# Slots of three SBUF pools set 4128 bytes apart instead of 4096

## The chip, the cores and the metric

The kernel runs on one core of a Trainium2 chip. The metric is device time in microseconds of one execution. The kernel before has a median of 1593.42 us over three runs.

## The reference

One layer of a streaming-encoder trunk for 512 tokens of width 1024. The parts that matter here:

```python
h    = rms_norm(x, norm_mix_gain)
proj = h @ w_in                              # 1024 x 3328, split into head groups
mixed = concat(stick_breaking(...), hgrn2(...), memory_attention(...))
x = x + mixed @ w_out
x = x + peer_ffn(rms_norm(x, norm_ffn_gain), ...)

def peer_ffn(h, w_query, sub_keys, expert_u, expert_v):   # per token, 8 heads
    q      = h @ w_query
    scores = einsum('bthcd,hcnd->bthcn', q, sub_keys)     # two lists of 128 keys
    top 16 of each list, top 16 of their sums -> expert_idx (of 16384), gate = softmax
    act = gelu(einsum('btd,bthkd->bthk', h, expert_u[expert_idx]))
    return einsum('bthk,bthkd->btd', gate * act, expert_v[expert_idx])
```

## The kernel before

The tokens lie in four tiles of 128. Tile 0 (`GT`) takes its experts by indirect DMA: 128 gathers of U rows and 128 of V rows. Tiles 1 to 3 (`DENSE`, 384 tokens) compute all 16384 experts densely, in 128 blocks of 128 experts: `u_mm` (line 1381) multiplies h2 by a block of U into the PSUM tile `ua`, and later `v_mm` (line 1456) multiplies the gated activations by a block of V into six PSUM banks `pin`.

Nearly every large product is made of three matmuls (`mm3`, line 419). Each float32 operand is split into a high part, rounded to the fp32r format by a copy, and a low part, the remainder: hi x hi, hi x lo and lo x hi are summed in PSUM. A U block (tile `ex`, 128x1024) is split by ScalarE into `xhi` and by VectorE into `xlo`; a V block likewise. The trace names a matmul's operands as moving operand first, stationary operand second: `ua<-h2hi,xhi` streams h2hi past the weights xhi, `pin<-xhi,whi` streams xhi past the weights whi.

SBUF tiles come out of tagged pools of equal slots (`slot`, line 284, and `t2`, line 302). The names that the change touches:

- `page`, tag "a2", 16 slots: gathered rows (`row`), gelu outputs (`gel`), one-hot tiles (`oh`), staging (`stg`), the running sum `xg`, and the early V splits.
- `hpage`, tag "h", 8 slots: the split activations (`hhi`, `hlo`, `mxh`, `mxl`, `h2hi`, `h2lo`).
- `wpage`, tag "w4", 8 slots: the split weights (`whi`, `wlo` of the projections; `xhi`, `xlo` of U and V blocks).

Not touched: `raw`, tag "raw", 7 slots (blocks as they land, `ex` and `w`); `t2`, 8 slots of 2048 bytes (`w`, `whi`, `wlo` of the gated activations, `shi` and `slo` of the stick-breaking part); `big3`, 2 slots (`G`); and the constants `ntri` and `nones`.

The program's list of allocations gives the byte addresses within a partition. In the kernel before, a2 starts at 20576, t2 at 86112, h at 102496, raw at 135264, w4 at 165984, b3 at 198816; the last tile ends at 228064. ntri lies at 17216 and nones at 18240. Modulo 4096, every a2, h and raw slot starts at 96, every w4 slot at 2144, and the t2 slots at 96 and 2144 in turn.

The order of the work is written out by the program: generators (`Threads`) are run against a clock model (`Pace`), and the engines take their instructions in the order in which the generators emit them. `Pace` reads an operand's tensor name and its offset within its tensor, not its address.

Of the kernel before, what the change touches and what calls it, by code (L numbers as in the profile page):

```python
# [20 lines left out]
P = 128  # L21
# [9 lines left out]

NPG, NRAW, NW4, NT2 = 16, 7, 8, 8
NBIG = 2
NSB = 3
QL = 2

# [228 lines left out]
def tile_trunk_layer(ctx: ExitStack, tc: tile.TileContext, x, mem, w_in, w_kv, w_out, w_query,  # L265
# [7 lines left out]
    sb = ctx.enter_context(tc.tile_pool(name="sb", bufs=1))  # L273
    ps = ctx.enter_context(tc.tile_pool(name="ps", bufs=1, space=PSUM))
    ctx.enter_context(tc.manual_schedule())
    uid = [0]

    def bank(name="pb", dt=F32, shape=None):
# [2 lines left out]
        PSUMS.add(b.tensor.name)  # L281
        return b

    def slot(tag, bufs):
        def make(shape, dt=F32, name="pg"):
            uid[0] += 1
            t = sb.tile(shape, dt, name=f"{name}{uid[0]}", tag=tag, bufs=bufs)
            return t
        return make

    page = slot("a2", NPG)
    hpage = slot("h", 8)
    wpage = slot("w4", NW4)
    raw = slot("raw", NRAW)
    big3 = slot("b3", NBIG)

# [1290 lines left out]

    for _ in range(NSB):
        th.add(sbreak())
# [66 lines left out]
```

## Time and profile before

| | us |
|---|---|
| median of three runs | 1593.42 (1592.74 to 1597.09) |
| the profiled execution's own time | 1591.55 |
| span of the profiled execution, first to last instruction | 1589.8 |
| TensorE busy | 1555.6 |
| VectorE busy | 1260.6 |
| ScalarE busy | 751.2 |
| mean granted TensorE clock, share of 2.4 GHz | 0.994 |

The profiled execution took 1.75 us more than its span, and 1.9 us less than the median. The time up to 472 us goes to projections, attention, recurrence, output projection and query; from 472 to 1059 us the U blocks run, with the top-k selection and the building of gate tables beside them; from 1059 to 1586 us the V blocks run. A line in the rows below, L204, is the helper that records every operation, so groups go by tiles. A matmul's duration in the rows contains its pipeline; the distance from one start to the next is what it takes of TensorE's time.

### The profile page before, as it was taken

Reading aid. Unit: us, or ns where it says so; the run is one execution under the profiler, and the core shown is the slowest. Engines: PE = TensorE matmul, PEld = TensorE weight load, DVE = VectorE, ACT = ScalarE, POOL = GpSimd, SP = SyncE. Lnnn points to the kernel's source line nnn. Section 1 sums busy time; section 2 is a strip of 40 time slices with the busy share of each in tenths; the row PEclk is TensorE's granted clock in tenths of the full one; section 3 lists DMA queues with packets and bytes.
Section 4 is the critical chain, followed back from the end, with each engine's and each line's share of the span. In section 5 each row is a group of like instructions: output and inputs, shape, how many; then the busy total and the mean of one; then the engine's idle time right before and its main releaser. Section 6 shows DMA issues by size and latency. Waiting matters only on the chain.

```text
span 1589.8 us, 25664 instructions
## 1 busy us (share of the span) xinstructions
PE 1555.6 (98%) x9359; PEld 1424.8 (90%) x9359; DVE 1260.6 (79%) x2527; ACT 751.2 (47%) x1427; POOL 351.9 (22%) x340
## 2 busy tenths in 40 slices
PE   6999998999999999999999999999999999999998
PEld 5998998889999999999999999988888888888887
DVE  5465568795887888788877878768898889888886
ACT  5422258854443456576566755533333333333332
POOL 3000000000061211121112110134344444344430
PEclk9999999999999999999999999999999999999999
DMA  6232102264297868889889898899999999999992
GB/s 252 80 106 80 54 28 89 97 226 135 86 336 260 267 224 297 272 290 319 263 280 299 277 295 262 296 402 408 408 408 407 395 377 382 387 390 380 364 380 77
DMA packets 163951, 422.72 MB, mean 266 GB/s; under 512 B 13552, under 2 KB 62704, under 8 KB 163824
## 3 DMA queue, kind: packets, MB, share of 16 engines
q1 hardware_dynamic: 67824, 236.51, 40.8%
q0 software_dynamic: 36864, 134.23, 23.0%
q10 hardware_dynamic: 59136, 50.34, 9.9%
q8 instruction: 73, 1.20, 0.3%
q14 instruction: 54, 0.44, 0.1%
HBM read 366.50 MB, written 54.53 MB: 265 GB/s over the span
## 4 chain that ended last, share of the span: by engine, by line
PE 93%; DVE 4%; ACT 2%; issue 1%; DMA 0%; SPq 0%; ACTq 0%; DVEq 0%
PE ua L204 34%; PE pin L204 33%; PE pf L204 5%; PE pt L204 4%; PE qf L204 4%; PE gb L204 3%; PE op L204 2%; PE hs L204 2%; PE qp L204 1%; PE sz L204 1%; ACT se L204 1%; PE qs L204 1%; DVE tka L204 1%; PE so L204 1%; PE nt L204 0%
## 5 line engine op out<-in xcount | busy, mean ns | idle before, releaser
L204 DVE TENSOR_TENSOR xlo<-ex,xhi 128x1024 fp32r<-128x1024 f32 x256 | 312.8, 1222 | 96.9 <-issue 45.1
L204 POOL DMA_INDIRECT row<-in_u_rows_dram,eidx x128 | 156.5, 1223 | 928.3 <-ACT sct L204 408.2
L204 PE MATMUL ua<-h2hi,xhi 128*128 128x384 f32 x1024 | 349.6, 341 | 0.0
L204 PE MATMUL ua<-h2hi,xlo 128*128 128x384 f32 x1024 | 343.5, 335 | 0.0
L204 PE MATMUL ua<-h2lo,xhi 128*128 128x384 f32 x1024 | 343.1, 335 | 0.0
L204 ACT ACTIVATE whi<-w 128x384 fp32r<-128x384 f32 (+1 forms) x201 | 141.0, 718 | 344.1 <-DVE w L204 325.2
L204 PE MATMUL pin<-xhi,whi 128*128 128x512 f32 x768 | 299.9, 390 | 1.5 <-ACT whi L204 1.5
L204 PE MATMUL pin<-xlo,whi 128*128 128x512 f32 x768 | 299.9, 391 | 1.2 <-DVE xlo L204 1.2
L204 PE MATMUL pin<-xhi,wlo 128*128 128x512 f32 x768 | 299.9, 391 | 0.0
L204 ACT ACTIVATE xhi<-ex 128x1024 fp32r<-128x1024 f32 x256 | 268.7, 1051 | 24.7 <-ACT stg L204 6.5
L204 DVE TENSOR_TENSOR wlo<-w,whi 128x384 fp32r<-128x384 f32 (+1 forms) x200 | 156.3, 796 | 110.7 <-ACT whi L204 56.7
L204 POOL DMA_INDIRECT row<-in_v_rows_dram,eidx x128 | 178.3, 1393 | 253.5 <-DVE w L204 129.2
L204 PEld LDWEIGHTS ua<-h2lo,xhi 128*128 128x128 f32 x1024 | 192.6, 188 | 0.0
L204 PEld LDWEIGHTS ua<-h2hi,xhi 128*128 128x128 f32 x1024 | 192.4, 188 | 0.0
L204 PEld LDWEIGHTS ua<-h2hi,xlo 128*128 128x128 f32 x1024 | 192.3, 188 | 0.0
L204 PEld LDWEIGHTS pin<-xhi,whi 128*128 128x128 f32 x768 | 144.7, 188 | 31.7 <-ACT whi L204 1.8
L204 PEld LDWEIGHTS pin<-xlo,whi 128*128 128x128 f32 x768 | 144.6, 188 | 31.5 <-DVE xlo L204 1.5
L204 PEld LDWEIGHTS pin<-xhi,wlo 128*128 128x128 f32 x768 | 144.6, 188 | 30.0
L204 DVE SCALAR_TENSOR_TENSOR xg<-row,wgt,xg 128x1024 f32<-128x1024 f32 x128 | 163.9, 1280 | 0.8
L204 DVE CUSTOM_DVE_ANT_0 row<-row,xr 128x1024 f32<-128x1024 f32 x128 | 155.2, 1218 | 4.6 <-DMA row<-in_u_rows_dram,eidx 4.6
L204 ACT ACTIVATE gel<-ua 128x384 f32<-128x384 f32 x128 | 62.8, 491 | 190.4 <-PE ua L204 189.2
L204 ACT ACTIVATE oh<-oh,gpg 128x128 f16<-128x128 f16 x256 | 84.3, 436 | 16.2 <-DVE sct L204 5.2
(255 smaller groups left out, 2281.1 us busy)
## 6 DMA issues: line engine op xcount, KB each, us to landing
ex<-in_u_t_dram SPq DMA_DIRECT2D x128, 512.0 KB, 4.7
ex<-in_v_rows_dram SPq DMA_DIRECT2D x128, 512.0 KB, 10.4
gel<-gel ACTq DMA_DIRECT2D x64, 384.0 KB, 4.1
gd<-stg ACTq DMA_DIRECT2D x48, 512.0 KB, 6.9
G<-gd SPq DMA_DIRECT2D x48, 512.0 KB, 6.9
gel<-gel SPq DMA_DIRECT2D x64, 384.0 KB, 9.9
w<-in_w_query_dram SPq DMA_DIRECT2D x28, 512.0 KB, 4.7
w<-in_w_in_dram SPq DMA_DIRECT2D x26, 512.0 KB, 4.9
```

The costliest lines, as they stand in the source:

```text
L204: r = fn(*args, **kw)
```

## The change

A slot of the pools a2, h and w4 is now a tile of 128 partitions x (4096 + 32) bytes. The tile that the caller asked for is the first part of it, reshaped to the caller's shape. Other pools stay as they were.

```diff
 NBIG = 2
+SLOT = 4096
 NSB = 3
...
+    PAD = {"w4": 32, "h": 32, "a2": 32}
+
     def slot(tag, bufs):
         def make(shape, dt=F32, name="pg"):
             uid[0] += 1
-            t = sb.tile(shape, dt, name=f"{name}{uid[0]}", tag=tag, bufs=bufs)
+            if tag not in PAD:
+                return sb.tile(shape, dt, name=f"{name}{uid[0]}", tag=tag, bufs=bufs)
+            n, z = 1, mybir.dt.size(dt)
+            for c in shape[1:]:
+                n *= c
+            t = sb.tile([P, SLOT // z + PAD[tag] // z], dt, name=f"{name}{uid[0]}", tag=tag, bufs=bufs)[:, :n]
+            if len(shape) > 2:
+                ax = "abcd"[:len(shape) - 1]
+                t = t.rearrange(f"p ({' '.join(ax)}) -> p {' '.join(ax)}", **dict(zip(ax[1:], shape[2:])))
             return t
         return make
```

The three pools have 32 slots together, so 1024 bytes of each partition are added.

## Rows read from the trace of the kernel before

**Rows 1.** From the page: busy time of each engine with its share of the span, and the chain of work that ended last, by engine and by line.

```profile
PE 1555.6 (98%) x9359; PEld 1424.8 (90%) x9359; DVE 1260.6 (79%) x2527; ACT 751.2 (47%) x1427; POOL 351.9 (22%) x340
...
PE 93%; DVE 4%; ACT 2%; issue 1%; DMA 0%; SPq 0%; ACTq 0%; DVEq 0%
PE ua L204 34%; PE pin L204 33%; PE pf L204 5%; PE pt L204 4%; PE qf L204 4%; PE gb L204 3%; PE op L204 2%; PE hs L204 2%; PE qp L204 1%; PE sz L204 1%; ACT se L204 1%; PE qs L204 1%; DVE tka L204 1%; PE so L204 1%; PE nt L204 0%
```

**Rows 2.** Busy time by stage, in three stretches: length, busy time of each engine with its instructions, then granted TensorE clock, DMA share (mean busy share of the 16 DMA engines) and GB/s.

```profile
0.00:472.00 472.00, 445.62 (x3199) 417.94 (x3200) 321.02 (x799) 230.61 (x456) 39.55 (x100) 0.99 0.37 129
472.00:1059.00 587.00, 585.58 (x3859) 572.97 (x3857) 475.36 (x1157) 332.75 (x716) 108.53 (x93) 1.00 0.85 284
1059.00:1586.00 527.00, 524.44 (x2304) 433.84 (x2304) 464.19 (x572) 187.86 (x256) 203.77 (x147) 1.00 0.95 369
```

**Rows 3.** What TensorE waited for from 472 to 1586 us: total us, times, longest.

```profile
PE pin L204 <- ACT whi L204: 1.5, 1, 1.5
PE pin L204 <- DVE xlo L204: 1.2, 1, 1.2
PE qs L204 <- ACT qT L204: 0.4, 1, 0.4
```

**Rows 4.** Groups of TensorE instructions with shapes kept apart: count, then busy us and mean ns of one. Each of the four stands for three groups of its name with the same count (hi x hi, hi x lo, lo x hi).

```profile
L204 PE MATMUL ua<-h2hi,xhi 128*128 128x384 f32 x1024 | 349.6, 341 | 0.0
L204 PE MATMUL pin<-xhi,wlo 128*128 128x512 f32 x768 | 299.9, 391 | 0.0
L204 PE MATMUL pf<-hhi,whi 128*128 128x512 f32 x128 | 50.8, 397 | 0.0
L204 PE MATMUL qf<-h2hi,whi 128*128 128x384 f32 x112 | 38.2, 341 | 0.0
```

**Rows 5.** Timeline of TensorE in the V blocks: start us, duration us. From the first of these rows to the last there are 15 matmuls, one to a row.

```profile
1399.63 0.39 PE L204 MATMUL pin<-xhi,whi 128*128 128x512 f32 x1
1399.86 0.39 PE L204 MATMUL pin<-xlo,whi 128*128 128x512 f32 x1
1400.08 0.39 PE L204 MATMUL pin<-xhi,wlo 128*128 128x512 f32 x1
...
1402.80 0.39 PE L204 MATMUL pin<-xhi,wlo 128*128 128x512 f32 x1
```

**Rows 6.** The same in the U blocks: 19 matmuls from the first row to the last.

```profile
699.73 0.34 PE L204 MATMUL ua<-h2lo,xhi 128*128 128x384 f32 x1
699.90 0.33 PE L204 MATMUL ua<-h2hi,xlo 128*128 128x384 f32 x1
700.08 0.34 PE L204 MATMUL ua<-h2hi,xhi 128*128 128x384 f32 x1
...
702.85 0.33 PE L204 MATMUL ua<-h2lo,xhi 128*128 128x384 f32 x1
```

**Rows 7.** Timeline of TensorE in the stick-breaking part: a matmul that streams slo past the constant ntri, and the one that follows at once with the constant nones. First two of the seven pairs with 512 columns that run back to back, then two of the six with 384 columns.

```profile
284.84 0.39 PE L204 MATMUL sz<-slo,ntri 128*128 128x512 f32 x1
285.07 0.39 PE L204 MATMUL sz<-slo,nones 128*128 128x128 f32 x2
...
305.10 0.39 PE L204 MATMUL sz<-slo,ntri 128*128 128x512 f32 x1
305.33 0.39 PE L204 MATMUL sz<-slo,nones 128*128 128x128 f32 x2
...
252.61 0.34 PE L204 MATMUL sz<-slo,ntri 128*128 128x384 f32 x1
252.78 0.40 PE L204 MATMUL sz<-slo,nones 128*128 128x128 f32 x2
...
269.03 0.34 PE L204 MATMUL sz<-slo,ntri 128*128 128x384 f32 x1
269.21 0.39 PE L204 MATMUL sz<-slo,nones 128*128 128x128 f32 x2
```

**Rows 8.** From the views by tile: duration in ns (shortest/median/longest), first and last start in us, and shape, of operations that read and write slots of the three pools, and of the weight loads of ua.

```profile
L204 DVE TENSOR_TENSOR xlo<-ex,xhi x256: 1205/1220/1300, 468.4 to 1572.9; 128x1024 fp32r<-128x1024 f32 x128
L204 ACT ACTIVATE xhi<-ex x256: 1039/1047/1089, 467.3 to 1571.0; 128x1024 fp32r<-128x1024 f32 x128
L204 DVE SCALAR_TENSOR_TENSOR xg<-row,wgt,xg x128: 1272/1280/1287, 1152.7 to 1575.3; 128x1024 f32<-128x1024 f32 x128
L204 PEld LDWEIGHTS ua<-h2hi,xhi x1024: 187/188/192, 472.7 to 1056.7; 128*128 128x128 f32 x171
L204 PEld LDWEIGHTS sz<-slo,ntri x32: 187/190/331, 173.0 to 309.3; 128*128 128x128 f32 x32
```

**Rows 9.** The DMA: from the page, the queue of the indirect gathers (packets, MB, share of 16 engines' span), and DMA issues with their size and median us to landing; then the gathers issued in the V stretch (POOL, x147), with the DMA share and GB/s of that stretch at the end of the line.

```profile
q0 software_dynamic: 36864, 134.23, 23.0%
ex<-in_v_rows_dram SPq DMA_DIRECT2D x128, 512.0 KB, 10.4
gel<-gel SPq DMA_DIRECT2D x64, 384.0 KB, 9.9
row<-in_v_rows_dram,eidx POOLq DMA_INDIRECT x128, 8.4
...
1065.00:1586.00 521.00, 195.83 (x155) 203.77 (x147) 1.00 0.95 368
```

**Rows 10.** What VectorE waited for from 1065 to 1586 us: total us, times, longest.

```profile
DVE wlo L204 <- PE pin L204: 50.5, 84, 1.1
DVE xr L204 <- PE pin L204: 4.8, 1, 4.8
```

## Prediction

> **What bounds the kernel now.** I read the page's busy times and its chain of waits first, then the stages, then TensorE's own waits, and last the distance between matmul starts. TensorE is busy for 98% of the span and makes up 93% of the chain that ended last; ua and pin alone are 67% of it [rows 1]. The stage view says the same of each stage: 585.6 of 587 us in the U blocks, 524.4 of 527 in the V blocks [rows 2]. In these 1114 us TensorE waited 3.1 us for anybody [rows 3]. So two questions decide this change: does the distance between two matmul starts move, and does some other engine or the DMA slow down so far that TensorE has to wait?
>
> **The distance now.** In the V blocks 14 steps take 1402.80 - 1399.63 = 3.17 us, 226.4 ns each [rows 5]. In the U blocks 18 steps take 3.12 us, 173.3 ns each [rows 6]. The 128 more columns cost 53.1 ns, 0.415 ns a column, which is the 2.4 GHz level of the clock. 512 columns are then 212.4 ns, and 14.0 ns of each matmul is a fixed part. That fixed part is all that a better layout could take from TensorE's stream. It is the same for whichever of the three products comes next, and for 384 and 512 columns within the 10 ns of the rows.
>
> **The change, part by part.**
>
> *Instructions.* None is added, removed or moved. The planner reads a tensor's name and offsets within a tensor; a view that starts at offset 0 of a slightly longer row gives it the same spans. Operands stay contiguous within a partition, so each keeps its shape and each DMA keeps its 4096-byte pieces. Cost 0. The three pools grow by 32 x 32 = 1024 bytes, to an end at 229088; no slot is given up for it.
>
> *Where operands lie.* Before, the starts of any two tiles in a2, h, w4, t2 and raw differ by multiples of 2048 bytes, and the slices that one matmul takes differ by multiples of 512. After, slot j of h and slot m of w4 differ, modulo 512, by 256 + 32(m - j): all sixteen phases occur. t2 moves by 512, raw by 768 and b3 by 1024 bytes as a whole. What this can change is a collision between two reads of one engine or between two engines, if such collisions depend on the phase.
>
> *TensorE, moving operand against weight load.* The trace before has matmuls at another phase. ntri and nones lie 736 and 1760 bytes past the phase of slo's slot, 224 modulo 512, which is 7 x 32 and one of the phases that the change brings in. With 384 columns six pairs start 0.17 or 0.18 us apart (mean 0.173), as in ua; with 512 columns seven pairs start 0.23 us apart against 0.226 [rows 7, 5, 6]. The weight load takes 188 ns for the ua blocks and 190 for ntri at the median [rows 8]. So the fixed part stands there too, undiminished. Bounds for the cost: below, the whole 14.0 ns goes away; above, the 3.6 ns by which the 512-column pairs stand over pin are real. Groups of three with 384 or 512 columns are 3 x (1024 + 768 + 128 + 112) = 6096 matmuls [rows 4]: 6096 x 14.0 = -85 us. Above: the 512-column ones are 3 x (768 + 128) = 2688, so 2688 x 3.6 = +10 us. I take 0, because the 384-column pairs are the nearest row and show no difference either way; a 512-column pair is followed by a 128-column matmul, not by its like.
>
> *VectorE and ScalarE.* Their operations on these slots meet every timing of TensorE's reads and of the DMA's writes, since the engines are not in step. If collisions cost anything at some phases, durations would spread. They don't: xg takes 1272 to 1287 ns over 128 times, xhi 1039 to 1089 and xlo 1205 to 1300 over 256 each [rows 8]. xlo reads two operands at one phase, xg reads two slots of one pool. The room for a gain is the median less the shortest, 15 ns x 256 for xlo, 4 us in all on an engine that waits for pin in 84 places [rows 10], so nothing at the end. Upward, VectorE is busy for 464 of 527 us in the V blocks [rows 2]: its operations could grow by 13% before it set the pace. The cover that hides them is this slack.
>
> *DMA.* Gathers and gelu tiles land in a2 at phases that now vary by slot. The DMA share in the V blocks is 0.95 [rows 2, 9], so the cover is thin. The moved transfers there are 147 gathers of 134.23 MB / 256 = 0.524 MB (77 MB) and 64 returns of gel of 0.393 MB (25 MB), against 521 us x 368 GB/s = 192 MB [rows 9]: 53%. The share reaches 1.0 when the moved transfers take 0.05 / 0.95 / 0.53 = 10% longer. The mean packet of the gather queue takes 0.23 x 16 x 1589.8 us / 36864 = 159 ns, index packets included [rows 9]; 10% is 16 ns on each. No row shows a transfer to another phase. I take 0: every slot stands at byte 96 modulo 256 before, and after it only one of every eight does, the others lying around it, so there is no aligned state to lose.
>
> The Trainium skill, page "DMA: Bandwidth & Descriptors", section "How a descriptor splits into AXI transactions", speaks against slots off a 256-byte boundary: transactions must start at such a boundary, and bytes below the start are fetched and dropped. By it, a 4096-byte piece at 96 modulo 256 counts 131 beats of 32 bytes, and the new slots count 128 to 135, 131.5 on average (an estimate from that page's rule). That would be 0.4% on the moved transfers, far below the 10% above, so by the rule the sum stays the same. The trace before, with one phase only, can't confirm it.
>
> **The sum.** 0 against the profiled execution's own 1591.55 us (span 1589.8 and 1.75 around it). Its three runs have a median 1.9 us above; against that median I forecast 1593.4 us.
>
> **The rivals.**
>
> *Faster: the fixed part is a collision.* If the 14 ns stand for weight loads and streams that meet because all starts are multiples of 512 apart, phases spread over sixteen values remove most of it. All of it gives 1593.4 - 85 = 1508; one tenth gives 1585. For it: the fixed part is the same everywhere, as a locked collision would be. Against it: ntri and nones at 224 modulo 512 show the same distance [rows 7].
>
> *Slower: phases that collide come in.* The mechanism is TensorE's two reads, in the V blocks and the first projections, 2688 matmuls of 512 columns. Price 3.6 ns each, +10 us, 1603. It decides against me from 1.8 ns each on (4.8 us, 0.3%). For it: the 0.23 us of the seven 512-column pairs. Against it: the 384-column pairs.
>
> *Slower: the DMA becomes the bound.* From 10% on the moved transfers. At 20% the share would be 0.95 x (1 + 0.53 x 0.20) = 1.05, 5% of 521 us, +26 us, 1619. For it: the share of 0.95. Against it: the phases before are no better ones.
>
> *The change does nothing to the addresses* (the allocator rounding slots to another step). The starts before are multiples of 32, so a step of 4128 can be given; if not, the time is again 1593.
>
> **How the numbers follow.** No change, including the last rival: 0.80. Faster collision: 0.10, spread from 1585 down to 1508. TensorE collision: 0.07. DMA: 0.03. Two measurements of this kernel can be told apart from about 0.3%, 4.8 us: 1588.6 to 1598.2. So faster 0.10, same 0.80, slower 0.10. The range takes in the forecast with its scatter and the priced slower bound: 1587 to 1603. Outside it lie the strong forms of the faster case and the DMA case, together under 2 in 10.
>
> **What would show it.** In the profile after, pin steps of 226 to 227 ns and ua steps of 173 to 174 ns would show the main step right; a pin step of 213 or one of 230 would show a rival, and so would a step that changes from block to block with the slot. Medians of xlo, xhi and xg more than 20 ns off would show the engines' reads do care. A DMA share near 1.0 in the V blocks, with landings far over 10 us and TensorE waiting for xhi or xlo, would show the DMA rival. A changed instruction count or new waits on TensorE would break the first step. I would be wrong above all if the phase matters only at differences other than 224 modulo 512, since the trace before holds only 0 and that one.

## The result, and the profile after

The changed kernel takes 1608.45 us (median of four runs, 1606.69 to 1610.27) against 1593.36 us (now also a median of four): a ratio of 1.009, 95% interval 1.0076 to 1.0104. That is 15.1 us slower, and outside the predicted range of 1587 to 1603. The forecast was no change.

Each engine has as many instructions as before (25664 in all), and from 472 us on TensorE waits for the same things; only addresses differ. So the two traces can be laid side by side stage by stage. The view by tile gives the first and the last start of the U and V matmuls; first the kernel before:

```profile
L204 PE MATMUL ua<-h2hi,xhi x1024: 333/335/424, 472.8 to 1056.9; 128*128 128x384 f32 x171
L204 PE MATMUL pin<-xhi,whi x768: 387/390/628, 1059.1 to 1583.9; 128*128 128x512 f32 x192
L204 PE MATMUL pin<-xhi,wlo x768: 388/390/629, 1061.1 to 1584.4; 128*128 128x512 f32 x192
```

and the same lines of the kernel after:

```profile
L205 PE MATMUL ua<-h2hi,xhi x1024: 331/337/427, 474.3 to 1062.9; 128*128 128x384 f32 x171
L205 PE MATMUL pin<-xhi,whi x768: 387/394/628, 1065.1 to 1600.7; 128*128 128x512 f32 x192
L205 PE MATMUL pin<-xhi,wlo x768: 387/393/628, 1067.4 to 1601.2; 128*128 128x512 f32 x192
```

From the first ua to the first pin it was 1059.1 - 472.8 = 586.3 us and is 1065.1 - 474.3 = 590.8, +4.5. From the first to the last pin it was 1584.4 - 1059.1 = 525.3 and is 1601.2 - 1065.1 = 536.1, +10.8. What lies ahead of the U blocks grew by 1.5 us, the tail not at all (5.4 us in both). Together 16.8 us, the difference of the two spans (1606.6 and 1589.8); the medians differ by less, 15.1, because the profiled execution of the kernel before was 1.8 us under its median. The V blocks carry two thirds of it.

What TensorE waited for from 472 to 1606 us in the kernel after:

```profile
PE pin L205 <- ACT whi L205: 1.5, 1, 1.5
PE pin L205 <- DVE xlo L205: 1.2, 1, 1.2
PE qs L205 <- ACT qT L205: 0.4, 1, 0.4
```

These are the same three waits as in [rows 3], to the tenth. Nobody keeps TensorE waiting for longer; its own matmuls follow one another more slowly. The timeline of the V blocks, 16 matmuls from the first row to the last, and of the U blocks, 11 matmuls (start us, duration us):

```profile
1399.98 0.39 PE L205 MATMUL pin<-xhi,whi 128*128 128x512 f32 x1
1400.21 0.39 PE L205 MATMUL pin<-xlo,whi 128*128 128x512 f32 x1
1400.45 0.39 PE L205 MATMUL pin<-xhi,wlo 128*128 128x512 f32 x1
...
1403.46 0.39 PE L205 MATMUL pin<-xhi,whi 128*128 128x512 f32 x1
```

```profile
701.08 0.34 PE L205 MATMUL ua<-h2lo,xhi 128*128 128x384 f32 x1
...
702.84 0.34 PE L205 MATMUL ua<-h2hi,xlo 128*128 128x384 f32 x1
```

15 steps of pin in 3.48 us are 232.0 ns each, against 226.4 in [rows 5]; 10 steps of ua in 1.76 us are 176.0 ns, against 173.3 in [rows 6]. The other engines and the DMA did not move. Durations by tile (shortest/median/longest, ns), then the stage view from 1059 to 1586 us, the V stretch of [rows 2], whose first 6 us are still U blocks here (DMA share and GB/s are the last two numbers):

```profile
L205 DVE TENSOR_TENSOR xlo<-ex,xhi x256: 1203/1219/1227, 469.9 to 1589.4; 128x1024 fp32r<-128x1024 f32 x128
L205 ACT ACTIVATE xhi<-ex x256: 1041/1047/1086, 468.8 to 1587.5; 128x1024 fp32r<-128x1024 f32 x128
L205 DVE SCALAR_TENSOR_TENSOR xg<-row,wgt,xg x128: 1274/1277/1286, 1160.0 to 1591.9; 128x1024 f32<-128x1024 f32 x128
L205 PEld LDWEIGHTS ua<-h2hi,xhi x1024: 187/188/192, 474.3 to 1062.7; 128*128 128x128 f32 x171
...
1059.00:1586.00 527.00, 524.26 (x2265) 425.18 (x2264) 453.77 (x560) 187.68 (x256) 207.38 (x149) 1.00 0.96 370
```

All stand within 3 ns of the medians in [rows 8]; the DMA has a share of 0.96 at 370 GB/s, against 0.95 and 369 in [rows 2]. Over the V blocks of this kernel alone, 1065 to 1601 us, the share is 0.93 at 360 GB/s: no more crowded than before. The weight loads last 188 ns as before.

### The profile page after: what moved, and what is told of

It is laid out like the page before. It is cut to its first block, busy times and chain, and to the rows that moved or that the text cites. A ratio compares the mean times of both kernels' runs of the same rounds, so it can differ in the third digit from the quotient of the medians.

```text
span 1606.6 us, 25664 instructions
## 1 busy us (share of the span) xinstructions
PE 1571.8 (98%) x9359; PEld 1427.8 (89%) x9359; DVE 1260.5 (78%) x2527; ACT 751.5 (47%) x1427; POOL 358.0 (22%) x340
## 4 chain that ended last, share of the span: by engine, by line
PE 93%; DVE 4%; ACT 2%; issue 1%; DMA 0%; SPq 0%; ACTq 0%; DVEq 0%
PE ua L205 34%; PE pin L205 33%; PE pf L205 6%; PE pt L205 4%; PE qf L205 4%; PE gb L205 3%; PE op L205 2%; PE hs L205 2%; PE qp L205 1%; PE sz L205 1%; ACT se L205 1%; PE qs L205 1%; DVE tka L205 1%; PE so L205 1%; PE nt L205 0%
## 5 line engine op out<-in xcount | busy, mean ns | idle before, releaser
L205 POOL DMA_INDIRECT row<-in_u_rows_dram,eidx x128 | 160.8, 1256 | 930.2 <-DVE tka L205 429.7
```

Source lines behind the costliest of these rows:

```text
L205: r = fn(*args, **kw)
```

## The experiments

**The theories.** A: the fixed part of an fp32r matmul's step (14 ns in the prediction) depends on the difference between the address of its stream and the address of the weights that are read beside it. The change spreads these differences over many values; before, those of all the large products were multiples of 512. B: each operand's own place counts. C: transfers and other engines working on a2 disturb TensorE. D, added later: the step of 4096 between slots is what matters.

**The phase table (run map_phase).** A kernel of its own, which leaves out the whole layer. One SBUF tile `B`, and chains of 32 equal matmuls:

```python
def group(name, n, mov, wt):
    b = ps.tile([P, 512], F32, name=name, tag="bank", bufs=8)
    for i in range(REP):
        nc.tensor.matmul(b[:, :n], B[:, wt // 4:wt // 4 + P], B[:, mov // 4:mov // 4 + n], ...)
    ...
...
for i in range(64): group("m" + letters(i), 512, 0, 4096 + 16 * i)
...
for i, s in enumerate((16, 32, 48, 64, 128)): group("both" + letters(i), 512, s, 4096 + s)
for i in range(32): group("n" + letters(i), 384, 0, 4096 + 16 * i)
for i in range(16): group("q" + letters(i), 256, 0, 4096 + 32 * i)
```

> This kernel computes nothing of the layer: it only times chains of 32 equal fp32r matmuls, with the weights at 4096 + delta bytes from the moving operand, delta from 0 to 1008 in steps of 16 with 512 columns, then 384 and 256 columns, and five chains in which both operands are shifted together. Theory A (the fixed part of a matmul depends on the address difference between its stream and the weights loaded beside it): the step is near 226.7 ns at delta 0, moves by several ns in both directions over delta, and stays as at delta 0 in the chains where both are shifted. Theory B (each operand's own alignment counts): the step at delta d equals that of the chain where both are shifted by d. Theory C (another engine or the DMA disturbs TensorE): all chains have one step, 226.7 ns, since nothing else runs here.

The timeline merges each chain into one row, so the distance from one chain's start to the next, over 32, is the step. `maa` to `map` are the differences 0 to 240 in steps of 16; `mba` is 256, `mbc` 288. In `bothab` stream and weights are both shifted by 32.

```profile
22.87 7.42 PE L38 MATMUL maa<-B 128*128 128x512 f32 x32
30.12 7.42 PE L38 MATMUL mab<-B 128*128 128x512 f32 x32
37.38 7.62 PE L38 MATMUL mac<-B 128*128 128x512 f32 x32
44.84 7.62 PE L38 MATMUL mad<-B 128*128 128x512 f32 x32
...
134.31 7.44 PE L38 MATMUL map<-B 128*128 128x512 f32 x32
141.59 7.42 PE L38 MATMUL mba<-B 128*128 128x512 f32 x32
148.84 7.42 PE L38 MATMUL mbb<-B 128*128 128x512 f32 x32
156.10 7.62 PE L38 MATMUL mbc<-B 128*128 128x512 f32 x32
163.56 7.62 PE L38 MATMUL mbd<-B 128*128 128x512 f32 x32
...
526.87 7.46 PE L38 MATMUL bothab<-B 128*128 128x512 f32 x32
534.17 7.53 PE L38 MATMUL bothac<-B 128*128 128x512 f32 x32
```

At difference 0 the step is (30.12 - 22.87) / 32 = 226.6 ns, at 16 it is 226.9; at 32 it jumps to (44.84 - 37.38) / 32 = 233.1. At 256 it is back at 226.6, at 288 again 233.1: the table repeats after 256 bytes, and the chains from 0 to 1008 hold four such periods that agree to 0.1 ns by the nanosecond starts of the trace. With both operands shifted by 32 it is (534.17 - 526.87) / 32 = 228.1 over the chain, of which the last twenty steps are 226.7: their own places do not matter in steps of 32. Nothing else ran, so C can't explain the 233. Chains at the multiples of 32 modulo 256, which are what slots 32 bytes apart produce (ns per step, weights less stream):

| difference | 0 | 32 | 64 | 96 | 128 | 160 | 192 | 224 |
|---|---|---|---|---|---|---|---|---|
| 512 columns | 226.6 | 233.1 | 233.4 | 234.1 | 233.4 | 233.4 | 233.4 | 233.1 |
| 384 columns | 173.3 | 173.8 | 173.1 | 176.6 | 175.9 | 176.9 | 173.4 | 173.4 |
| 256 columns | 120.0 | 118.1 | 117.8 | 117.5 | 120.0 | 120.0 | 117.8 | 117.8 |

(The rows print starts to 10 ns, so an entry is good to 0.3 ns. 384 columns at 0: the end of the chain, 173.3; its first eight steps are 177.) The mean of the first line is 232.6, of the second 174.6. With 512 columns every phase in this line other than 0 costs; with 256 columns most phases gain. Theory A had expected steps that move both ways with 512 columns too; none fell below the step at 0.

**One pool at a time.** The edit is the list of padded pools:

```diff
-    PAD = {"w4": 32, "h": 32, "a2": 32}
+    PAD = {"w4": 32}      # only_w4; only_h and only_a2 likewise
```

> Only the pool w4 has slots 4128 apart. Theory A: the weights of the U blocks and the streams of the V blocks are in w4, so both stages keep about the steps of the full change, ua near 175.5 and pin near 232 ns, and the time is 1604 to 1610. Theory B: about the same, as the same operands are misplaced. Theory C: less than half of the loss, 1593 to 1600, because gathered rows and gel tiles lie as before.

> Only the pool h has slots 4128 apart. Theory A: ua steps near 175.5 ns and shorter steps in the 256-column matmuls, pin back at 226.7 ns; 1597 to 1602. Theory B: the same direction, with ua up by the part that its stream's own alignment costs. Theory C: 1593, since no transfer goes to that pool.

> Only the pool a2 has slots 4128 apart. Theory A: hardly any matmul of the split products has an operand there, so ua stays at 173.3 and pin at 226.7 ns, 1593 (1590 to 1596). Theory B: the same. Theory C (gathers, gel tiles and their neighbours in a2 cause the loss): 1604 to 1610, with pin steps near 232 ns.

Measured: only_w4 1611.74 us, ratio 1.0115 (1.0098 to 1.0132); only_h 1598.27 us, 1.0027 (1.0017 to 1.0038); only_a2 1592.43 us, 0.9996 (0.9987 to 1.0006). The last pin start and the first, by tile: 1604.3 - 1068.0 = 536.3 us with w4 alone, 1589.6 - 1064.3 = 525.3 with h alone, 1584.9 - 1061.3 = 523.6 with a2 alone. The lines that show it, of only_w4, only_h and then only_a2:

```profile
L205 PE MATMUL pin<-xhi,whi x768: 387/394/632, 1068.0 to 1603.9; 128*128 128x512 f32 x192
L205 PE MATMUL pin<-xhi,wlo x768: 387/393/632, 1070.3 to 1604.3; 128*128 128x512 f32 x192
```

```profile
L205 PE MATMUL pin<-xhi,whi x768: 389/389/628, 1064.3 to 1589.1; 128*128 128x512 f32 x192
L205 PE MATMUL pin<-xhi,wlo x768: 388/389/628, 1066.4 to 1589.6; 128*128 128x512 f32 x192
```

```profile
L205 PE MATMUL pin<-xhi,whi x768: 389/389/505, 1061.3 to 1584.5; 128*128 128x512 f32 x192
L205 PE MATMUL pin<-xhi,wlo x768: 388/389/398, 1063.4 to 1584.9; 128*128 128x512 f32 x192
```

The loss sits in w4, as the stream of the V blocks, with a smaller part in h, whose U blocks take 1064.3 - 474.8 = 589.5 us, 3.2 more than before. The parts don't add up: w4 alone costs 18.4 us (1.7 us over the range expected for it) and h alone 5.0, while all three pools together cost 15.1. That fits a cost that goes by the difference of two addresses, since the U blocks and the projections take one operand from each of these pools. C falls: the pool that takes all the gathers costs nothing when it alone is padded.

**A shift without a new step.** In the next four kernels all slots stay 4096 bytes apart. An unused tile ahead of a pool moves the whole pool:

```diff
             w = self.raw[s]
+            if s == 0:
+                sb.tile([P, 8], F32, name="gapw", tag="gapw", bufs=1)
             h = wpage([P, 4, 256], F32R, name="whi")
```

(8 elements for 32 bytes, 24 for 96, 64 for 256; shift_w4_t2 has in addition 32 bytes ahead of t2 and 224 ahead of h, so that t2 and w4 lie 32 bytes further modulo 256 and h as before.)

> The kernel before with one unused tile of 32 bytes ahead of w4: all slots stay 4096 apart, and w4 lies 32 bytes further. Theory A with the measured table of phases (weights less stream, modulo 256): pin at phase 224 goes from 226.7 to 233.35 ns (2304 x 6.7 = +15.4 us), pf at 32 to 233.35 (384 x 6.7 = +2.6), ua and qf at 32 stay at 173.3, the 256-column matmuls at 224 go from 120.0 to 117.8 (1224 x -2.2 = -2.7): 1608.6 (1605 to 1612). Theory D (the step between slots matters, 4096 being a good one): 1593.

> The same with a tile of 96 bytes ahead of w4. Theory A: pin at phase 160 233.45 ns (+15.6 us), ua and qf at 96 176.65 ns (3408 x 3.35 = +11.4), pf at 96 234.15 (+2.9), the 256-column ones at 160 unchanged: +29.9, 1623 (1618 to 1628), twice the loss of the full change with slots 4096 apart. Theory D: 1593.

> The same with a tile of 256 bytes ahead of w4. Theory A: the table repeats after 256 bytes, so pin 226.7 and ua 173.3 ns and 1593 (1590 to 1596). If the place of w4 itself or the distance between pools counted, this would move like the other shifts, to 1600 or more.

> w4 and t2 both lie 32 bytes further (modulo 256), h and a2 as before, so that w4 against t2 is at phase 0 again and w4 against h at 32. Theory A: pin back at 226.7, ua 173.3, pf 233.35 (+2.6 us), the 256-column ones 117.8 (-2.7): 1593 (1590 to 1596). Theory B (each operand's own place counts): as bad as the shift of w4 alone, 1608.

| kernel | us | ratio (95%) | ua stage, us | pin stage, us |
|---|---|---|---|---|
| shift_w4_32 | 1609.50 | 1.0102 (1.0085 to 1.0119) | 585.5 | 540.3 |
| shift_w4_96 | 1607.63 | 1.0086 (1.0070 to 1.0103) | 585.1 | 538.9 |
| shift_w4_256 | 1593.24 | 0.9997 (0.9988 to 1.0007) | 586.3 | 523.7 |
| shift_w4_t2 | 1592.23 | 0.9991 (0.9982 to 1.0001) | 585.4 | 526.4 |

The stages run from the first ua to the first pin, and from there to the last pin, as above; before they were 586.3 and 525.3. Pin stages can be compared to about 1.6 us only, unless one looks at the clock: TensorE waits for 1.5 and 1.2 us at the head of the V blocks, and in some of the runs the granted clock falls right after that. In the kernel before it was 0.50 of full speed from 1063 to 1065 us, the 1.2 GHz level, with pin steps of 427 ns; the kernel after and shift_w4_32 have such a stretch too, and shift_w4_t2 a longer one. In shift_w4_96, shift_w4_256 and only_a2 the clock stayed at 1.00. Moving w4 by 32 bytes, with the old step between slots, costs as much as the whole change: 15.0 us in the V blocks where the table gave 15.4. (In the projections pf went from 227 to 233.5 ns a step, and the 256-column steps from 120 to 117, at the median, as the table has it.) Moving it by 256 costs nothing, and moving t2 along with it takes the loss away again. So D falls, and B too: w4 lies as far off in shift_w4_t2 as in shift_w4_32. The lines of shift_w4_t2 that show it, and the timeline of shift_w4_32, in which 12 steps of pin take 2.81 us, 234 ns each:

```profile
L204 PE MATMUL pin<-xhi,whi x768: 389/389/632, 1058.5 to 1584.5; 128*128 128x512 f32 x192
L204 PE MATMUL pin<-xhi,wlo x768: 388/389/632, 1060.8 to 1584.9; 128*128 128x512 f32 x192
```

```profile
1399.98 0.39 PE L204 MATMUL pin<-xhi,whi 128*128 128x512 f32 x1
1400.22 0.40 PE L204 MATMUL pin<-xlo,whi 128*128 128x512 f32 x1
...
1402.79 0.39 PE L204 MATMUL pin<-xhi,whi 128*128 128x512 f32 x1
```

One expectation missed by far. shift_w4_96 was to take 1623 us, with 11 us of it from ua and qf at 176.65 ns; it took 1607.6, and ua stayed as fast as before (585.1 us). The pin stage did what the table says: 538.9 us against 523.7 in shift_w4_256, two runs without the stretch at the low clock, is +15.2, expected +15.6.

**Order or history (run map_order).** Does the table for 384 columns fail because a U block takes its addresses in another order than the chains? This kernel times three kinds of chains, each after a chain at phase 0:

```python
...
for i in range(8):
    chain("uz", 384, u(0)); chain("u" + letters(2 * i), 384, u(32 * i))          # order of a U block
for i in range(8):
    chain("nz", 384, [(H, W)] * 48); chain("n" + letters(2 * i), 384, [(H, W + 32 * i)] * 48)  # one pair of addresses
for i in range(8):
    chain("vz", 512, v(0)); chain("v" + letters(2 * i), 512, v(32 * i))          # order of a V block
```

(`u(ph)` and `v(ph)` list pairs of addresses, of the stream and of the weights, as a U and a V block take them, with the weights ph bytes off phase 0; `H` and `W` are two places in `B`, 32768 bytes apart.)

> This kernel computes nothing of the layer: it times chains of 48 matmuls, each after a chain at phase 0. Chains u take the addresses in the order of a U block (two streams, two weights, eight steps, 384 columns), chains v in the order of a V block (512 columns), chains n repeat one pair of addresses with 384 columns; phases 0 to 224 in steps of 32. Theory A, table alone: u equals n at each phase, 176.65 ns at 96 and at 160, and v is 233 to 234 ns at all phases but 0. Theory A with the order counting: n is 176.65 ns at 96 as in the first table, while u is 173.3 ns at 96, as the U blocks were in the kernel with w4 shifted by 96; v near 233.3 at 160 and 224.

The u and n chains at 64 (`uae`, `nae`) and 96 (`uag`, `nag`), each with the chain at phase 0 that follows:

```profile
72.22 8.64 PE L37 MATMUL uae<-B 128*128 128x384 f32 x48
80.70 8.48 PE L37 MATMUL uz<-B 128*128 128x384 f32 x48
89.03 8.49 PE L37 MATMUL uag<-B 128*128 128x384 f32 x48
97.35 8.51 PE L37 MATMUL uz<-B 128*128 128x384 f32 x48
...
206.04 8.64 PE L37 MATMUL nae<-B 128*128 128x384 f32 x48
214.51 8.48 PE L37 MATMUL nz<-B 128*128 128x384 f32 x48
222.84 8.49 PE L37 MATMUL nag<-B 128*128 128x384 f32 x48
231.17 8.51 PE L37 MATMUL nz<-B 128*128 128x384 f32 x48
```

At 64 the step is (80.70 - 72.22) / 48 = 176.7 ns for u and 176.5 for n; at 96 it is 173.3 and 173.5. So the order of addresses makes no difference, and the expectation that blamed it falls. But the first table had 173.1 at 64 and 176.6 at 96, where each chain came after its neighbour 16 bytes below; so the expectation by the table alone misses as well. The same difference has more than one steady step. What decides between them was not tested by itself: between the two runs the chain that ran just before is another, but so are the length of the chains and the distance from stream to weights, 32768 bytes against 4096. Chains u, which cover many distances, agree with n, and this speaks against the distance. With 512 columns 192 was far from the first table, (471.68 - 459.31) / 54 = 229.1 ns, and 128 a little below it; 32, 64, 96, 128 and 160 gave 233.1, 233.3, 234.3, 232.6 and 233.3.

## Why the prediction was wrong

*Instructions and waits: right.* Same counts, and TensorE's three waits of 3.1 us behind 472 us came back unchanged.

*VectorE, ScalarE, DMA: right.* Medians moved by 3 ns at most, the DMA share by 0.01; only_a2 measured the pool of the gathers by itself at 0.9996. The rule of the Trainium skill, page "DMA: Bandwidth & Descriptors", section "How a descriptor splits into AXI transactions", would have cost little by the prediction's estimate, and only_a2 shows no cost; with so small an estimate this neither bears out the rule nor speaks against it.

*TensorE, moving operand against weight load: wrong.* This is the step that failed. The prediction named the mechanism in its second rival, "phases that collide come in", priced it at 3.6 ns on 2688 matmuls, +10 us, and gave it 7%. The term that it set at 0 measured 10.8 us in the V blocks and 4.5 in the U blocks. Two things were off.

First, the evidence against it. I read one other phase out of the trace, 224 modulo 512, and took it for all. The table shows what that phase is: with 384 columns it is one that can run free (173.4 ns in the first table; 176.7 in map_order, after a chain at phase 0), and the row that I called the nearest happened to. With 512 columns it is a dear one, 233.1. The seven pairs at 0.23 us [rows 7] pointed that way, and I set them aside because a matmul of another length follows. To the nanosecond they start 229.4 ns apart on average (228 to 232), 2.7 more than pin; a chain at that phase pays 6.5. That they show the cost of the chain, in single matmuls between others, is argued and not shown. The prediction did name this way to be wrong in its last sentence, but only for differences other than 224; the sign that it gave for a rival, a pin step of 230 ns, came as 232.

Second, the size. pin pays 10.8 us / 2303 = 4.7 ns per step, not 3.6. That is still less than the table gives: its mean over the eight phases, 232.6 less 226.6, is 6.0 ns, 13.8 us. By the starts in the trace, steps at the low clock left out, the mean step in the kernel after changes from block to block, from 230.9 to 232.5 ns over the four pairs of slots. xhi and xlo of a block lie in slots of their own, so the phase changes from product to product; no chain did that, and why the mixture costs less than its parts stays open. In shift_w4_32, where the phase is constant, the step is the chain's 233.3. And ua, which I priced at 0, pays 4.5 us / 3071 = 1.5 ns, about the table's mean of 174.6 less 173.3. The 256-column matmuls give a little back: 118 ns a step at the median, 120 before. Put into the prediction's own sum, 2304 x 4.7 + 3072 x 1.5 = 15.4 us where it had +10 at most: 1609, against 1608.45 measured. Both prices are read off the kernel after, so the sum tells where the time went and is no test of the table.

The bound below, "the fixed part is a collision", fell as well: no phase brought a step of 384 or 512 columns below 173 or 226.6 ns for a whole chain. The layout before already sat on the best phase for its products with 384 and 512 columns. Nor did an experiment point to a better one: shift_w4_t2, where the 256-column matmuls gain and pf loses, is level with the kernel before.

The Trainium skill, page "TensorE: Matmul & The Clock Gate", section "Part 2: What happens when you issue a matmul", says that the stream and the weight load have a read port of SBUF each, and: "Loading the next tile's weights doesn't steal SBUF read bandwidth from the running matmul." By it this change would cost TensorE nothing. The runs differ: the same chain takes 226.6 or 233.1 ns a step with 32 bytes of difference between the two addresses, and the measurement decides.

One count of the prediction is off without bearing on the result: modulo 512 the change brings in fifteen phases, not sixteen, since m - j runs from -7 to 7; modulo 256, which matters, all eight occur.

What stays open: why 256 bytes, which read gives way, and whether a stream meets the load of its own weights or of the next matmul's. That the stream stalls on the weight load is argued from the dependence on the difference alone; no run here has a matmul without a weight load of its own. What picks one of the several steady steps at a phase is not known; that it is the preceding chain is likely but untested.

## What to carry to other kernels

Keep the moving and the stationary operand of fp32r matmuls with 512 columns at the same place modulo 256 bytes, or at least check the step between starts after any change of layout, even one that moves no instruction. When a trace is to rule out an address effect, one other phase is not a sample: a chain of matmuls over all phases took one run and gave the answer that no row of the kernel held. Such a chain shows that a cost exists and gives its size where the phase is constant; for ua at 96 (expected 176.65 ns, no loss measured) and for the mixed phases of pin it was no price list. And where rows disagree, as the 384- and the 512-column pairs did here, price the term with the shape that carries most of the time.

## What the runs showed of the hardware

An fp32r matmul's step depends on the address difference between weights and stream with a period of 256 bytes: 226.6 to 234.1 ns with 512 columns, 173.1 to 176.9 with 384, 117.5 to 120.0 with 256, where phase 0 is the best for the first two (with 384 columns some others equal it) and among the worst for the last. Shifting both operands together by 32, 64 or 128 bytes leaves the step at 226.7 ns in the end; by 16 or 48 bytes it is 230.0. At the same difference a chain with 384 columns can settle at 173.3 or 176.7 ns; between the two runs that show it the chain that ran before was another, but not that alone.
